# Matrix products of ones in TensorE's first waits, and three constant loads moved behind the tokens, in a two-layer hybrid decoder

## The chip, the cores and the metric

The kernel runs on one core of a Trainium2 chip. The metric is the device time of one execution in microseconds. A core has five engines that run their own instruction streams and wait for each other on semaphores: TensorE (PE in the profile; its weight loads have a row of their own, PEld), VectorE (DVE), ScalarE (ACT), GpSimd (POOL) and SyncE (SP). Copies between the memory of the device and the core are issued by SP, ScalarE or GpSimd and carried out by 16 DMA engines.

## The reference

Two layers of a decoder with 512 tokens behind 16 learned meta tokens, so 528 columns, and a model width of 1024. Each layer normalises its input, projects it, runs two kinds of heads side by side (forgetting attention, and retention with a fixed decay per head), joins them in an output projection, and ends with a gated feed-forward block:

```python
xn = rmsnorm(h, attn_norm_g)
proj = jnp.einsum('bld,dc->blc', xn, w_in)
fq, fk, fv, flog, rq, rk, rv, rg = jnp.split(proj, SPLIT_POINTS, axis=-1)
logf = jax.nn.log_sigmoid(flog.astype(jnp.float32) + b_fgate.astype(jnp.float32))
fox_out = fox_attention(fq.reshape(fshape), fk.reshape(fshape), fv.reshape(fshape), logf)
...
h = h + jnp.einsum('blc,cd->bld', mix, w_out)
hn = rmsnorm(h, ffn_norm_g)
ff = jax.nn.silu(jnp.einsum('bld,df->blf', hn, w_gate)) * jnp.einsum('bld,df->blf', hn, w_up)
return h + jnp.einsum('blf,fd->bld', ff, w_down)
```

Everything is float32. The change concerns the first 25 us or so of layer 0: the loads of the tokens, the first products of the input projection, the forget gates (`flog`) and the sum of squares of the norm.

## The kernel before, in words

**Layout.** The tokens stand transposed in eight tiles `h[0]` to `h[7]` of 128 features x 528 tokens. Weights come in tiles of 128 x 8 x 128, 512 KB each. To keep float32 accuracy with a faster number format, each operand is split into a high part and a low part (`xh`, `xl` of the tokens, `whi`, `wlo` of the weights), and each product is made of three: high by high, high by low, low by high (line 200). A product covers 264 columns, so there are six of them for each k (the 128 features) and each output tile. ScalarE makes the high parts (`xh` at line 298, `whi` at 176), VectorE or GpSimd the low ones (`xl` at 299, `wlo` at 177).

**The start of layer 0.** `start` (line 1096) issues all on SP: token tile 0, the first quarter of the two first weight tiles (those of q and k of the first pair of attention heads), token tile 1, the second quarter, token tiles 2 and 3, the other half of both weight tiles, token tiles 4 to 7. `scale_split` (line 290) then splits the tokens. Before that, at lines 52 to 59, four small constants are loaded: `idt` (a 128 x 128 identity for transposes) and `msk` (a 128 x 128 causal mask), 64 KB each, and `bfg` (the bias of the forget gates, 8 x 2) by GpSimd, and `vec` (norm weights) by ScalarE. `ones` (128 x 128) is written by VectorE at line 61; it serves as the weight operand that sums squares over the features.

**The order on TensorE** is written out by hand; `plan` is a list of steps, and `run(plan)` emits them under a manual schedule for TensorE alone. For layer 0 (line 1118) it alternates q and k: `qk[0]` is k = 0 of the q tile, `qk[1]` k = 0 of the k tile, and so on. After the first six of them come the squares of the tokens (`squares`, line 303; no TensorE work), then k = 3 to 6, then the forget gates (`forget_gates`, line 350: 32 products at line 360, with a split weight tile `pth` made from `wfr`), then the sums of squares (`col_rstd`, line 266: four products with `ones` at line 273, their results `R`), then `forget_sums` (line 369, which reads `bfg`, first through `nbfg` at line 373), and last k = 7. The v tile follows.

**The other engines** are ordered by the scheduler of the framework, which places every instruction by its own estimate of when its operands are there; an operand that arrives later moves its reader back in the stream of its engine. SP and GpSimd issue their DMAs in program order.

**PSUM.** `psum_a()` hands out four banks of 512 columns in turn, `psum()` two pairs.

Of the kernel before, what the change touches and what calls it, by code (L numbers as in the profile page):

```python
# [38 lines left out]
def hybrid_kernel(ctx, tc, x_t, w_in, w_fl, w_out, w_gate, w_up, w_down, vecs, b_fg, rope, decay, mask, ident, out_t):  # L39
    nc = tc.nc  # L40
# [9 lines left out]
    h = [state.tile([128, T], F32, name=f"h{k}") for k in range(NK)]  # L50

    idt = const.tile([128, 128], F32, name="idt")
    nc.gpsimd.dma_start(idt, ident)
    msk = const.tile([128, 128], F32, name="msk")
    nc.gpsimd.dma_start(msk, mask)
    vec = const.tile([128, vecs.shape[1]], F32, name="vec")
    nc.scalar.dma_start(vec, vecs)
    bfg = const.tile([FH, DEPTH], F32, name="bfg")
    nc.gpsimd.dma_start(bfg, b_fg)
    ones = const.tile([128, 128], F32R, name="ones")  # L60
    nc.vector.memset(ones.bitcast(F32), 1.0)
    epsc = const.tile([128, 1], F32, name="epsc")
# [35 lines left out]

    def zero(l, t):
        (nc.gpsimd if l else nc.vector).memset(t, 0.0)  # L100

    def take(lst, key):
        t = lst[rot[key] % len(lst)]
        rot[key] += 1
        return t
# [17 lines left out]
    def vcol(c):  # L123
        return vec[:, c:c + 1]
# [11 lines left out]
    def fetch(j):  # L136
        job = jobs[j]
        if "load" in job:
            job["load"]()
        elif "raw" not in job:  # L140
            n = job["src"].shape[1]
            job["raw"] = wp.tile([128, NK, 128], F32, name="raw", tag="raw", bufs=3)
            if j > 1:
                nc.sync.dma_start(job["raw"], job["src"]) if n == NK else \
                    nc.sync.dma_start(job["raw"][:, 0:n], job["src"])
# [96 lines left out]
    def psum_a():  # L242
        return psa.tile([128, 512], F32, name="psa", tag="psa")
# [5 lines left out]
    def tt(name, dt=F32):  # L249
        tag, bufs = tags[name]  # L250
        return tmp.tile([128, T], dt, name=name, tag=tag, bufs=bufs)

    def at(tag, dt=F32R, shape=(128, T), bufs=None):
        return phase["att"].tile(list(shape), dt, name=tag, tag=tag, bufs=bufs)
# [4 lines left out]
    def col_parts(src, cols):  # L259
        c_all = slice(cols[0][0], cols[-1][1])  # L260
        sh = tt("sqh", F32R)
        sl = tt("sql", F32R)
        split(sh[:, c_all], sl[:, c_all], src[:, c_all])
        return sh, sl
# [22 lines left out]
    FULL = ((0, HALF), (HALF, T))  # L287
    REAL = ((META, T),)

    def scale_split(st, gcol, cols):  # L290

        c = slice(cols[0][0], cols[-1][1])
        st["x"] = []
        for k in range(NK):
            xh = state.tile([128, T], F32R, name=f"xh{k}", tag=f"xh{k}")
            xl = state.tile([128, T], F32R, name=f"xl{k}", tag=f"xl{k}")
            g = vcol(gcol + k)
            nc.scalar.activation(xh[:, c], h[k][:, c], AF.Copy, scale=g)
            nc.vector.scalar_tensor_tensor(xl[:, c], h[k][:, c], g, xh[:, c].bitcast(F32),  # L299
                                           ALU.mult, ALU.subtract)  # L300
            st["x"].append((xh, xl))

    def squares(st, cols, pinned=False):
        c = slice(cols[0][0], cols[-1][1])
        acc = tt("ss")
        for k in range(NK):
            if k == 0:
                first = nc.scalar.activation(acc[:, c], h[0][:, c], AF.Square)
                if pinned:
                    tc.keep_in_program_order(first)  # L310
            else:
                sq = tt("sq")
                nc.scalar.activation(sq[:, c], h[k][:, c], AF.Square)
                nc.vector.tensor_add(acc[:, c], acc[:, c], sq[:, c])
        st["parts"] = col_parts(acc, cols)
# [23 lines left out]
    def rstd(st, cols, rname="R"):  # L339

        st["R"] = col_rstd(st["parts"], D, cols, rname)
# [27 lines left out]
    def forget_sums(l, st):  # L369
        z = st["z"]  # L370
        z2 = tt("z2")[0:FH]
        nbfg = tmp.tile([FH, 1], F32, name="nbfg", tag="nbfg")
        nc.vector.tensor_scalar_mul(nbfg, bfg[:, l:l + 1], -1.0)
        nc.vector.scalar_tensor_tensor(z, z, RSC, st["R"][0:FH, :], ALU.mult, ALU.mult)
        nc.scalar.activation(z2, z, AF.Abs, bias=bfg[:, l:l + 1])
        nc.scalar.activation(z2, z2, AF.Exp, scale=-1.0)
        nc.scalar.activation(z2, z2, AF.Ln, bias=onec[0:FH])
        nc.scalar.activation(z, z, AF.Relu, scale=-1.0, bias=nbfg)
        nc.vector.tensor_add(z, z, z2)
        nc.vector.tensor_tensor_scan(z2, z, z, 0.0, ALU.add, ALU.max)  # L380
        st["cdr"] = tc.dram_tile([FH, T], F32, name=f"cdr{l}")
        nc.sync.dma_start(st["cdr"], z2)
# [687 lines left out]
    def layer(l):  # L1070

        real = l == DEPTH - 1
        QC = REAL if real else FULL
        ly, ff = {}, {}
        fox = [{} for _ in range(FP)]
        ret = [{} for _ in range(RH)]

        def ropes():
            for i, n in enumerate(("cr", "sr")):
                t = at(n, F32)  # L1080
                nc.sync.dma_start(t, rope[i])
                nc.vector.scalar_tensor_tensor(t, t, RSC, ly["R"], ALU.mult, ALU.mult)
                ly[n] = t

        def fd(g):
            return fox_dense(l, g, ly, real, fox[g])

        def rd(hd, which):
            return ret_dense(l, hd, ly, real, ret[hd], which)

        mixes = [[fox[0], ret[0], fox[1], ret[1]], [fox[2], ret[2], fox[3], ret[3]]]
        fs = [fox_steps(g, fox[g], ly, real) for g in range(FP)]
        rs = [ret_steps(l, hd, ret[hd], real) for hd in range(RH)]
        plan = []

        def start():
            if l == 0:
                pieces = {0: (0, 2), 1: (2, 4), 3: (4, NK)}
                for k in range(NK):
                    nc.sync.dma_start(h[k], x_t[k])  # L1100
                    if k in pieces:
                        for j in range(2):
                            fetch(j)
                            c = slice(*pieces[k])
                            nc.sync.dma_start(jobs[j]["raw"][:, c], jobs[j]["src"][:, c])
            scale_split(ly, V_ATTN + l * NK, FULL)

        def start_ffn():
            scale_split(ff, V_FFN + l * NK, QC)

        q, k, v = fd(0)
        qk = [f for pair in zip(q, k) for f in pair]
        stats = [lambda: rstd(ly, FULL)]
        gates = [lambda: forget_gates(l, ly)]
        sums = [lambda: forget_sums(l, ly)]
        plan = [lambda: enter_att(l), start]
        if l == 0:
            plan += qk[:6] + [lambda: squares(ly, FULL, True)] + qk[6:-2] + gates + stats + sums + qk[-2:]
        else:
            plan += [lambda: squares(ly, FULL)] + q[:7] + stats + q[7:] + gates + sums + k  # L1120
        plan += v + [ropes]

        def ret_places(hd, *places):

            f = rs[hd]
            return list(zip(places, (f[0], f[1], f[2], f[4], f[3], f[5], f[6], f[7], f[8], f[9])))

        for g in range(2):
            main, rest = fs[g]
            m0, r0, places = (((7, 31), (34, 40.5), (13, 33.5, 35.5, 37.5, 39, 40.5, 43, 44, 47.5, 48)),  # L1130
                              ((0.5, 31.5), (32, 40), (13, 33.5, 35.5, 39.5, 39, 41.5, 43, 44, 47.5, 48)))[g]
            plan += merge(rd(g, "vqkg") + sum(fd(g + 1), []),
                          spread(main, *m0), spread(rest, *r0), ret_places(g, *places))
        main, rest = fs[2]
        op = out_proj(l, 0, mixes[0], real)
        op[:8] = op[0:3] + op[4:7] + [op[3], op[7]]
        plan += merge(op + sum(fd(3), []), spread(main, 4, 30.5), spread(rest, 32, 42))
        main, rest = fs[3]
        base = rd(2, "qkv") + rd(3, "qkv") + rd(2, "g") + rd(3, "g")
        op = out_proj(l, 1, mixes[1], real)  # L1140
        base += op[0:3] + op[4:7] + op[8:11] + op[12:15]
        plan += merge(base, spread(main, 2, 46.5), spread(rest, 51, 56),
                      ret_places(2, 26, 22.5, 23.5, 32, 28, 33.5, 36, 56.5, 40.5, 57.5),
                      ret_places(3, 52, 45.5, 47.5, 57.5, 55.5, 58.5, 60, 64.1, 63, 64.2))
        plan += [op[3], op[7], op[11], op[15]] + op[16:]
        up = ffn(l, ff, real, real)
        plan += [lambda: enter("ffn"), start_ffn] + up
        return plan

    plan = [f for l in range(DEPTH) for f in layer(l)]  # L1150
# [76 lines left out]
```

## Time and profile before

| | us |
|---|---|
| median of 3 runs | 1300.8 |
| lowest and highest | 1298.96, 1301.67 |
| profiled execution | 1302.07 |
| its span, first to last instruction | 1300.3 |
| TensorE busy in the span | 1271.6 |

The profile is of one execution. Its span is 1.8 us shorter than its time; what lies outside is start and end of the execution. A line of the timeline gives the start in us, the busy time, engine, source line, operation, output and inputs, shapes and count; instructions of one group that follow each other are merged, and in brackets stands the idle time ahead of them and what ended it. "PEq", "SPq" and so on are the sequencers, which issue DMAs and branch. In the chain that ended last, each line is a start, a length and who carried the chain in that time. In a table of windows, PEclk is the clock that was granted to TensorE, as a share of full speed. DMA queue q1 is the one of SP, q10 the one of ScalarE, and q0 (software) the one of GpSimd.

### The profile page before, as it was taken

The numbers are of one execution on the slowest core, as the hardware profiler recorded it, in microseconds if no ns is written. First come the engines' busy times: TensorE is split into PE (matmuls) and PEld (weight loads), VectorE is DVE, ScalarE is ACT, GpSimd is POOL, SyncE is SP. The second block draws the span as 40 slices with busy tenths as digits, with TensorE's granted clock in tenths as the row PEclk, the third lists the DMA queues.
The fourth block names the chain that finished last, engine by engine and source line by source line (L and its number), as shares of the span: only waits on it lengthen the run. The fifth ranks groups of instructions, "written<-read, shape, count | busy, mean of one in ns | idle before, by whom it ended". The sixth has DMA issues, their size and how long they took to land.

```text
span 1300.3 us, 23291 instructions
## 1 busy us (share of the span) xinstructions
PE 1271.6 (98%) x9326; PEld 1210.3 (93%) x9326; DVE 1005.5 (77%) x1827; ACT 706.7 (54%) x1277; POOL 192.7 (15%) x157
## 2 busy tenths in 40 slices
PE   8999999999999999999999999999999999999996
PEld 7999999999999999999998989988789999999995
DVE  7877756869988777777786767568899888888866
ACT  6776555576444444444466665457764444444444
POOL 3332333230000000000013324333200000000000
PEclk9999899999999999999999999999999999999998
DMA  5322222213333333332323222222224333333321
GB/s 196 107 76 72 74 82 82 60 55 122 103 110 98 98 98 98 98 98 82 102 71 115 74 82 82 77 87 66 97 81 129 99 98 97 98 111 103 96 65 65
DMA packets 45468, 120.54 MB, mean 93 GB/s; under 512 B 5376, under 2 KB 12032, under 8 KB 45360
## 3 DMA queue, kind: packets, MB, share of 16 engines
q1 hardware_dynamic: 45120, 118.90, 29.1%
q8 instruction: 73, 1.20, 0.4%
q14 instruction: 35, 0.29, 0.1%
q0 software_dynamic: 96, 0.13, 0.1%
q10 hardware_dynamic: 144, 0.02, 0.0%
HBM read 116.91 MB, written 2.13 MB: 92 GB/s over the span
## 4 chain that ended last, share of the span: by engine, by line
PE 82%; DVE 9%; ACT 6%; issue 1%; DMA 1%; POOL 0%; SPq 0%; DVEq 0%; ACTq 0%; POOLq 0%
PE psd L200 23%; PE psa L823 17%; PE psd L958 14%; PE psd L823 13%; PE psa L200 5%; PE psa L958 4%; PE psa L396 2%; PE psa L480 1%; PE psa L687 1%; PE psa L540 1%; DVE xl L299 1%; ACT whi L176 1%; PE psa L657 1%; DVE tq L585 1%; DVE ptl L129 1%
## 5 line engine op out<-in xcount | busy, mean ns | idle before, releaser
L177 POOL TENSOR_TENSOR wlo<-raw,whi 128x512 fp32r<-128x512 f32 x136 | 186.8, 1388 | 399.5 <-ACT whi L176 396.6
L200 PE MATMUL psd<-xh,whi 128*128 128x264 f32 (+1 forms) x792 | 198.0, 318 | 5.1 <-ACT whi L176 4.7
L200 PE MATMUL psd<-xh,wlo 128*128 128x264 f32 (+1 forms) x792 | 188.1, 305 | 0.4 <-POOL wlo L177 0.4
L200 PE MATMUL psd<-xl,whi 128*128 128x264 f32 (+1 forms) x792 | 188.0, 305 | 0.0
L200 PEld LDWEIGHTS psd<-xh,whi 128*128 128x128 f32 x792 | 130.2, 192 | 9.6 <-ACT whi L176 4.7
L200 PEld LDWEIGHTS psd<-xh,wlo 128*128 128x128 f32 x792 | 128.7, 191 | 6.5 <-POOL wlo L177 0.6
L200 PEld LDWEIGHTS psd<-xl,whi 128*128 128x128 f32 x792 | 129.3, 191 | 4.2 <-DVE xl L299 0.3
L176 ACT CAST whi<-raw 128x512 fp32r<-128x512 f32 (+1 forms) x170 | 99.6, 613 | 34.4 <-issue 17.8
L811 ACT CAST whi<-raw 128x1024 fp32r<-128x1024 f32 (+2 forms) x62 | 54.9, 885 | 49.8 <-PE psd L823 37.5
L811 ACT CAST fwhi<-raw 128x1024 fp32r<-128x1024 f32 (+2 forms) x62 | 55.7, 898 | 47.4 <-PE psd L823 39.7
L812 DVE TENSOR_TENSOR wlo<-raw,whi 128x1024 fp32r<-128x1024 f32 (+2 forms) x62 | 62.8, 1013 | 11.5 <-ACT whi L811 11.4
L812 DVE TENSOR_TENSOR fwlo<-raw,fwhi 128x1024 fp32r<-128x1024 f32 (+2 forms) x62 | 63.9, 1031 | 9.0 <-ACT fwhi L811 8.6
L823 PE MATMUL psa<-tl,whi 128*128 128x264 f32 (+1 forms) x232 | 65.8, 284 | 0.0
L823 PE MATMUL psa<-th,whi 128*128 128x264 f32 (+1 forms) x232 | 65.8, 284 | 0.0
L823 PE MATMUL psa<-th,wlo 128*128 128x264 f32 (+1 forms) x232 | 65.7, 283 | 0.0
L823 PE MATMUL psa<-th,fwhi 128*128 128x264 f32 (+1 forms) x224 | 63.6, 284 | 0.0
L823 PE MATMUL psa<-th,fwlo 128*128 128x264 f32 (+1 forms) x224 | 63.5, 283 | 0.0
L823 PE MATMUL psa<-tl,fwhi 128*128 128x264 f32 (+1 forms) x224 | 63.4, 283 | 0.0
L499 ACT ACTIVATE pdNone<-pdNone,nmax 128x144 f32<-128x144 f32 (+1 forms) x64 | 37.0, 577 | 47.9 <-DVE nmax L486 35.7
L129 DVE TENSOR_TENSOR ptl<-psa,pth 128x512 fp32r<-128x512 f32 (+4 forms) x88 | 41.8, 490 | 23.3 <-ACT pth L128 23.1
L811 ACT CAST fwhi<-S 128x1024 fp32r<-128x1024 f32 x20 | 21.0, 1051 | 69.7 <-PE psa L823 66.3
L889 ACT COPY e<-psa 128x264 f32<-128x264 f32 (+1 forms) x114 | 42.8, 375 | 27.7 <-PE psa L823 23.8
(311 smaller groups left out, 4035.7 us busy)
## 6 DMA issues: line engine op xcount, KB each, us to landing
raw<-w_in SPq DMA_DIRECT2D x54, 512.0 KB, 3.5
raw<-w_gate SPq DMA_DIRECT2D x44, 512.0 KB, 3.9
fraw<-w_up SPq DMA_DIRECT2D x38, 512.0 KB, 3.5
raw<-w_down SPq DMA_DIRECT2D x64, 256.0 KB, 2.9
raw<-w_out SPq DMA_DIRECT2D x16, 512.0 KB, 3.6
raw<-w_down SPq DMA_DIRECT2D x32, 192.0 KB, 2.5
bc<-cdr SPq DMA_DIRECT2D x16, 264.0 KB, 3.5
raw<-w_up SPq DMA_DIRECT2D x6, 512.0 KB, 3.4
```

The lines of the kernel that those rows point to most:

```text
L129: nc.vector.tensor_sub(lo, src, hi.bitcast(F32))
L176: nc.scalar.copy(hi, job["raw"][:, c0:c1])
L177: sub(lo, job["raw"][:, c0:c1], hi.bitcast(F32))
L200: nc.tensor.matmul(ps[1][b][:, 0:c1 - c0], w[:, wk, :], x[:, c0:c1], start=(k == 0 and i == 0), stop=(k == n - 1 and i == 2))
L299: nc.vector.scalar_tensor_tensor(xl[:, c], h[k][:, c], g, xh[:, c].bitcast(F32), ALU.mult, ALU.subtract)
L396: nc.tensor.transpose(ps[:, 128 * j:128 * j + 128], src[:, o:o + 128], idt)
L499: nc.scalar.activation(pr, pr, AF.Exp, bias=nmax[0:nq], scale=-1.0, accum_out=rsum)
L811: nc.scalar.copy(hi, src)
L812: nc.vector.tensor_sub(lo, src, hi.bitcast(F32))
L823: nc.tensor.matmul(bank()[:, 0:b.shape[-1]], a[:, o + k, :], b, start=(fresh and k == 0 and i == 0), stop=(k == n - 1 and i == 2), skip_gr ...
L889: nc.scalar.copy(self.t["e"][:, i], self.t["x"][:, 0:w])
L958: nc.tensor.matmul(v[:, 0:c1 - c0], a[:, s * n + k, :], b[:, c0:c1], start=(k == 0 and i == 0), stop=(k == n - 1 and i == 2))
```

## The change

Two things. First, a helper `keep_warm(n)` emits n products of `ones` by `ones`, 128 x 128 by 128 columns, into a PSUM bank of their own that nothing reads. 32 of them stand at the head of TensorE's stream, 16 between k = 0 and k = 1, and 4 between k = 1 and k = 2. Second, the loads of `idt`, `msk` and `bfg` leave GpSimd and the head of the program, and are issued by SP behind the eighth token tile, in the order `bfg`, `msk`, `idt`.

```diff
     idt = const.tile([128, 128], F32, name="idt")
-    nc.gpsimd.dma_start(idt, ident)
     msk = const.tile([128, 128], F32, name="msk")
-    nc.gpsimd.dma_start(msk, mask)
     vec = const.tile([128, vecs.shape[1]], F32, name="vec")
     nc.scalar.dma_start(vec, vecs)
     bfg = const.tile([FH, DEPTH], F32, name="bfg")
-    nc.gpsimd.dma_start(bfg, b_fg)
...
+    idle = []
+
+    def keep_warm(n):
+
+        if not idle:
+            idle.append(psum_a())
+        for _ in range(n):
+            nc.tensor.matmul(idle[0][:, 0:128], ones, ones, start=True, stop=True)
...
         def start():
             if l == 0:
+                keep_warm(32)
                 pieces = {0: (0, 2), 1: (2, 4), 3: (4, NK)}
...
+                for t, src in ((bfg, b_fg), (msk, mask), (idt, ident)):
+                    nc.sync.dma_start(t, src)
             scale_split(ly, V_ATTN + l * NK, FULL)
...
-            plan += qk[:6] + [lambda: squares(ly, FULL, True)] + qk[6:-2] + gates + stats + sums + qk[-2:]
+            plan += qk[:2] + [lambda: keep_warm(16)] + qk[2:4] + [lambda: keep_warm(4)] + qk[4:6] + [lambda: squares(ly, FULL, True)] + qk[6:-2] + gates + stats + sums + qk[-2:]
```

In the streams of the changed kernel, TensorE has the 52 products at these three places and is otherwise as before. GpSimd loses the three issues, SP gains them between the last token tile and the load of `wfr` (line 352). On VectorE the two `nbfg` (line 373) move from behind the first low weight part to between the additions of the squares (line 314); ScalarE's order is the same.

## The prediction

> **What bounds the kernel now.** I read the page first, then the waits and the chain of the first 45 us, then the timeline. The page's busy line and the shares of the chain that ended last:
>
> ```profile
> PE 1271.6 (98%) x9326; PEld 1210.3 (93%) x9326; DVE 1005.5 (77%) x1827; ACT 706.7 (54%) x1277; POOL 192.7 (15%) x157
> ...
> PE 82%; DVE 9%; ACT 6%; issue 1%; DMA 1%; POOL 0%; SPq 0%; DVEq 0%; ACTq 0%; POOLq 0%
> ```
>
> TensorE carries the span. The change touches only the first 24 us, so the question is by how much the work behind that point starts earlier or later. TensorE's longest wait from 0 to 45 us (total, times, longest), and the chain over the start:
>
> ```profile
> PE psd L200 <- ACT whi L176: 4.7, 1, 4.7
> ```
>
> ```profile
> 2.15 5.21 DMA h<-x_t
> ...
> 8.17 11.40 PE psd L200 x72
> 19.57 3.80 PE psa L360 x31
> ...
> 24.12 0.85 ACT R L278 x2
> ```
>
> The second token tile lands at 7.36 us. From 8.17 on TensorE itself is the chain: 72 products (k = 1 to 6), the forget gates (L360), the four sums of squares (L273). From 24.12 on ScalarE and VectorE carry it for a while (R, then q, k and the cumulated gates), and TensorE waits for them now and then. So whatever moves the L273 products moves all that follows by the same amount. In the timeline, the next product behind them starts at 23.79; that is my reference point.
>
> ```profile
> 0.83 0.17 DVE L61 MEMSET ones<- 128x128 f32 x1 [0.83 <-PEq L1215]
> ...
> 4.71 0.81 PE L200 MATMUL psd<-xh,whi 128*128 128x264 f32 x2 [4.71 <-ACT whi L176]
> ...
> 11.78 0.64 PE L200 MATMUL psd<-xl,whi 128*128 128x264 f32 x2
> ...
> 12.22 0.64 PE L200 MATMUL psd<-xh,wlo 128*128 128x264 f32 x2
> ...
> 13.08 0.41 PE L200 MATMUL psd<-xl,whi 128*128 128x264 f32 x2
> ...
> 13.33 0.40 PE L200 MATMUL psd<-xh,wlo 128*128 128x264 f32 x2
> ...
> 23.79 0.41 PE L200 MATMUL psd<-xh,whi 128*128 128x264 f32 x2
> ```
>
> Two products of 264 columns take 0.44 us before 12.9 us and 0.245 us after 13.1: 0.22 against 0.122 each. The array runs at half pace until about 13 us, and the released pace is what the added products are to bring forward.
>
> **The added products.** 32 stand ahead of the first real product, 16 behind the twelve of k = 0, 4 behind the twelve of k = 1. Each loads 128 columns of `ones` and streams 128. TensorE works in order, so the real ones wait for them. The trace has no such product; its nearest rows are 128-column transposes, at full and at half pace (each row asked for where one starts):
>
> ```profile
> 128.92 0.49 PE L396 MATMUL psa<-idt,pdNone 128*128 128x128 f32 x3
> 129.03 0.49 PE L396 MATMUL psa<-idt,pdNone 128*128 128x128 f32 x3
> ```
>
> ```profile
> 137.18 0.63 PE L548 MATMUL psa<-idt,tq 128*128 128x128 f32 x2
> 137.39 0.63 PE L548 MATMUL psa<-idt,tq 128*128 128x128 f32 x2
> ```
>
> Starts lie 0.11 us apart at full pace and 0.21 at half. By columns alone it would be 128/264 of 0.122 and 0.22, so 0.059 and 0.107; the weight load sets the pace. Products of 16 columns with a full weight load show it too:
>
> ```profile
> 133.49 0.28 PE L692 MATMUL psa<-rsh,rvh 128*128 128x16 f32 x1 [0.80 <-DVE ptl L129]
> 133.62 0.26 PE L692 MATMUL psa<-rsl,rvh 128*128 128x16 f32 x1
> ```
>
> (0.13 apart.) I take 0.11 and 0.213; the lower end, 0.107 at half pace, is kept for a rival. The Trainium skill (TensorE: Matmul & The Clock Gate, section on LDWEIGHTS) gives a load as its columns over 1.2 GHz whatever the clock, so 107 ns for 128 columns; the rows at full pace agree, those at half pace (0.21) do not, and by the page 32 products would end at 4.5 us and not at 7.9.
>
> **Do they release the clock?** This decides the case. The granted clock was 0.5 in one stretch in mid kernel, 135.9 to 142.7. The window just before it, two others, and the stretch itself (length; PE, PEld, DVE, ACT, POOL busy and count; PEclk; DMA):
>
> ```profile
> 132.50:135.91 3.41, 2.40 (x16) 2.07 (x15) 2.87 (x9) 1.60 (x4) 2.27 (x2) 1.00 0.59 177
> 770.80:774.20 3.40, 2.11 (x11) 1.15 (x9) 0.77 (x2) 3.33 (x6) 0.00 (x0) 1.00 0.48 154
> ...
> 6.21:9.62 3.41, 3.02 (x13) 2.41 (x12) 2.04 (x8) 2.23 (x5) 0.00 (x0) 1.00 1.03 370
> ```
>
> ```profile
> 135.90:142.70 6.80, 5.99 (x28) 5.88 (x27) 4.52 (x7) 2.19 (x6) 0.48 (x1) 0.50 0.34 108
> ```
>
> The stretch is 6.8 us long, twice 3.4, and begins 122.9 us, 36 times 3.41, behind the change of pace at 13.0: I read it as a decision every 3.41 us on the stretch just past, in a grid that does not start with the kernel. The clock fell behind the first window, in which PE and weight loads were busier (2.40, 2.07) than in the second (2.11, 1.15), where it held. Busy time and loads do not decide. Streamed columns do:
>
> ```profile
> L540 PE MATMUL psa<-pth,vv x5: 218/286/467, 134.4 to 135.7; 128*128 128x512 f32 x1, 128*128 128x400 f32 x1, 128*128 128x272 f32 x1, 128*128 128x144 f32 x1
> L540 PE MATMUL psa<-ptl,vv x5: 275/287/392, 134.7 to 135.8; 128*128 128x512 f32 x1, 128*128 128x400 f32 x1, 128*128 128x272 f32 x1, 128*128 128x144 f32 x1
> ```
>
> ```profile
> L200 PE MATMUL psd<-xh,whi 128*128 128x512 f32 x2 | 0.9, 437 | 0.0
> L200 PE MATMUL psd<-xh,wlo 128*128 128x512 f32 x2 | 0.8, 397 | 0.0
> L200 PE MATMUL psd<-xl,whi 128*128 128x512 f32 x2 | 0.8, 396 | 0.0
> L396 PE MATMUL psa<-idt,pdNone 128*128 128x128 f32 x4 | 0.7, 286 | 1.2 <-DVE sd L662 1.2
> ```
>
> The first window streams twice 1,344 columns (the fifth form has 16) and a few of 16, about 2,770; the second 6 x 512 + 4 x 128 less what began before it, about 3,300. At the start, 6.21 to 9.62 begins 11 products of 264, at most 2,900 columns, and the pace stayed at half (the PEclk column reads 1.00 there, but the pairs still take 0.44). At half pace 16 added products fit into 3.41 us: 16 x 128 = 2,050 columns, fewer than in any of these that fell or stayed. **So I take it that the added products alone do not release it**; dense real ones do (15 x 264 = 4,100 columns in 3.41 us).
>
> **The sum.** TensorE starts at 1.05, when `ones` is written. 32 x 0.213 = 6.8, so k = 0 starts at 7.9 and not at 4.71; its tokens and weights are there. 12 x 0.22 = 2.6: 10.5. Two paths from here. *Early*: these twelve release the clock at about 11.4. Of 16 added, 4 run at 0.213 and 12 at 0.11: 12.7. Then 12 x 0.122: 14.2; 4 x 0.11: 14.6; 60 x 0.122 for k = 2 to 6: 21.9; 32 x 0.122 for the gates: 25.8; 4 for the sums: 26.3. Against 23.79 that is 2.5 us later. *Late*: the added 16 dilute it, all run at 0.213 (13.9), and k = 1 releases it at about 15.9: 9 x 0.22 and 3 x 0.122 give 16.3, and the same rest (0.44 + 7.3 + 3.9 + 0.5) gives 28.4, 4.6 later. When in the 3.4 us grid the kernel starts is open, so both occur; between them, nearer the early one, I take 3.5 us later.
>
> **The moved loads.** Three software issues leave POOL; SP takes them behind the eighth token tile.
>
> ```profile
> q0 software_dynamic: 93, 0.13, 29.1%
> ```
>
> ```profile
> 3.00:4.00 1.00, 0.00 (x0) 0.00 (x0) 0.80 (x8) 0.37 (x1) 1.00 (x2) 1.00 1.10 224
> 4.00:5.00 1.00, 0.29 (x1) 0.29 (x2) 0.71 (x10) 0.66 (x2) 0.00 (x0) 1.00 0.72 180
> ...
> 6.00:7.00 1.00, 1.00 (x7) 1.00 (x6) 0.45 (x2) 0.04 (x1) 0.00 (x0) 1.00 1.04 361
> ```
>
> From 3 to 6 us the software queue took 29% of the engines' time, 0.87 us, and from 3 to 5 DMA moved 224 and 180 GB/s where it later moves 361. Without it the second token tile lands 0.9 to 2 us earlier. On my paths that is worth nothing: TensorE is not through the added products before 7.9, and ScalarE and VectorE are ahead of it from then on. If the added products were short, it would count in full (rival 2). The price of the move lies elsewhere:
>
> ```profile
> 6.98 0.14 DVE L373 TENSOR_SCALAR nbfg<-bfg 8x1 f32<-8x1 f32 x1 [0.49 <-DMA bfg<-b_fg]
> ...
> 8.75 0.52 SPq L352 DMA_DIRECT2D wfr<-w_fl  x1
> 9.44 3.37 SPq L144 DMA_DIRECT2D raw<-w_in  x2
> ...
> 16.64 0.23 ACT L128 CAST pth<-wfr 128x64 fp32r<-128x64 f32 x1
> ...
> 21.90 0.71 DVE L129 TENSOR_TENSOR sql<-ss,sqh 128x528 fp32r<-128x528 f32 x1 [0.70 <-ACT sqh L128]
> ```
>
> Three issues on SP at some 0.45 us move `wfr` from 8.75 to about 10.1; before, it was read 7.9 us after its issue, so it bears this, and the weight load that stands behind it waits in any case until 12.5 for a buffer. The two `nbfg` (0.14 each) move on VectorE between the additions of the squares: `sql` is ready at 22.9 instead of 22.6, and queued behind them are only those additions, L273's operands. L273 comes at 25.8, so 3 us of TensorE work cover it; without that cover it costs 0.3 us. Mask and identity serve the attention, behind R at 24.12. The other orders on VectorE, ScalarE and SP are unchanged, the spare PSUM bank makes no engine wait.
>
> **Rivals.**
> 1. *The added products do release the clock*, though they stream half the time. By mechanism: TensorE is never idle from 1.05 on, so the first whole window of 3.41 us ends between 4.5 and 7.9, and releases it. The 32 then end at 6.2 to 7.9; 12 x 0.122, 16 x 0.11, 12 x 0.122, 4 x 0.11, 60, 32 and 4 x 0.122 add 16.8: 23.0 to 24.7, that is 0.8 earlier to 0.9 later. Not slower: about 1300.8. For it: PE and weight loads without a gap. Against it: the two windows above. 22%. The Trainium skill (same page, Part 1 on the clock gate) states this rule: about 3.4 us of sustained issue release the clock, in a free-running window, whatever the number of products; the grid agrees with the rows here, that being busy suffices does not.
> 2. *Faster: the added products are short*, 0.107 at half pace. They end at 4.5, before the first operand, and the earlier tokens count. The real work then waits for VectorE: `sql` at 22.9 less 0.9 to 2, then four products; 0.9 to 2.6 us earlier, 1298.2 to 1299.9. It decides from the point where 32 of them take under 3.6 us (0.113 each). Against it: 0.21 in the L548 rows. 11%.
> 3. *No release before k = 2*: all through k = 1 and the 4 at half pace (17.4), release at about 22.2, 31.3 at the reference: 7.5 later, 1308.3. For it: 3.4 us with 2,050 columns on both sides of the twelve. 18%.
>
> **How the numbers follow.** The profiled execution took 1302.07 us (span 1300.3 and 1.8 around it), 1.3 above the median 1300.8; the half-pace stretch near 136 may be part of that, and it need not come in every run. I add the difference to the median: 1300.8 + 3.5 = **1304.3**, chance 46%, its own range 1302.8 to 1305.9. The remaining 3% is the unforeseen. The range from 1299.8 to 1308.6 takes in rivals 1 and most of 3, and the near end of 2. A difference of 0.2%, 2.6 us, is about what a measurement of this kernel can tell from no change. Slower by more: 30 of my 46 (the rest are early releases under 2.6), 18 of rival 3 and 2 of the rest, 50%. Faster by more: 5 of rival 2, and 5 for rivals 1 and 2 with a lucky clock in mid kernel, 10%. Within: 40%.
>
> **What would show it.** Right: 32 products of `ones` about 0.21 apart, the first L200 at 7.9, pairs at 0.44 through k = 0, release at 11 to 16, the first L200 behind L273 at 26 to 28.5. Wrong: pairs at 0.25 already in k = 0 (rival 1), the added ones 0.11 apart from the start (rival 2). The second token tile should land 0.9 to 2 us earlier with q0 empty, and nobody wait for `wfr`, `bfg`, mask or identity.

## The result, and the profile after

| | before | after |
|---|---|---|
| median of 16 runs each, side by side | 1300.11 us | 1303.16 us |
| lowest and highest | 1298.39, 1302.43 | 1301.44, 1306.04 |
| profiled execution, its span | 1302.07, 1300.3 | 1301.44, 1299.6 |

The ratio of after to before is 1.0026, with a 95% interval of 1.0019 to 1.0033. The changed kernel is 3.05 us slower, where 3.5 was forecast. (The 16 runs of before include the three from which 1300.8 came.)

The spans of the two profiled executions say the opposite: after's is 0.7 us shorter. The stage of the change must be read by itself. Here is TensorE's timeline after, over the first 26.5 us, with the lines that answer to those shown of before (L206 was L200, L279 was L273, L106 is the new helper):

```profile
1.05 7.09 PE L106 MATMUL psa<-ones 128*128 128x128 f32 x32 [1.05 <-DVE ones L58]
7.94 0.75 PE L206 MATMUL psd<-xh,whi 128*128 128x264 f32 x2
...
10.69 2.02 PE L106 MATMUL psa<-ones 128*128 128x128 f32 x16
12.54 0.46 PE L206 MATMUL psd<-xh,whi 128*128 128x264 f32 x2
...
14.05 0.56 PE L106 MATMUL psa<-ones 128*128 128x128 f32 x4
...
25.93 0.40 PE L279 MATMUL psa<-sql,ones 128*128 128x264 f32 x2
26.17 0.41 PE L206 MATMUL psd<-xh,whi 128*128 128x264 f32 x2
```

The 32 products take from 1.05 to 7.94, 0.215 each. The twelve of k = 0 take from 7.94 to 10.69, 0.229 each: still half pace. The 16 then take only 1.85 us, so the pace changes at their first or second (one at 0.213 and the rest at 0.11), at 10.9. The reference point, the first L206 behind the sums of squares, comes at 26.17 and not at 23.79: **2.4 us later**.

Where did the profiled execution get that back? The next two fences are the transposes near 137 us, where ScalarE had kept TensorE waiting, and the product behind that stage, first after, then before:

```profile
139.28 0.66 PE L554 MATMUL psa<-idt,tq 128*128 128x128 f32 x4 [0.83 <-ACT d L699]
...
143.46 0.49 PE L206 MATMUL psd<-xh,whi 128*128 128x264 f32 x2
```

```profile
136.91 1.12 PE L548 MATMUL psa<-idt,tq 128*128 128x128 f32 x4 [0.81 <-ACT d L693]
...
143.73 0.49 PE L200 MATMUL psd<-xh,whi 128*128 128x264 f32 x2
```

At the transposes after is still 2.37 us late, the whole of the 2.4. At the product behind them it is 0.27 early. Between them lies the stretch of 6.8 us in which before ran at half pace. The same window after:

```profile
135.90:142.70 6.80, 5.76 (x42) 5.53 (x43) 5.65 (x12) 3.53 (x9) 1.71 (x2) 1.00 0.55 190
```

The granted clock is 1.00 there. Before's profile lost 2.6 us to a fall of the clock that this execution was spared. Such falls come and go: in the profiles of the kernels below, one stood at 134.5, 136.8 or 142.2 us, or near 770, or there was none. So the two spans cannot be compared, and only the medians and the reference point can.

### The profile page after: what moved, and what is told of

Same layout as the page of the kernel before. It is cut to its first block, busy times and chain, and to the rows that moved or that the text cites. A ratio compares the mean times of both kernels' runs of the same rounds, so it can differ in the third digit from the quotient of the medians.

```text
span 1299.6 us, 23394 instructions
## 1 busy us (share of the span) xinstructions
PE 1275.3 (98%) x9378; PEld 1214.7 (93%) x9378; DVE 1006.1 (77%) x1827; ACT 706.8 (54%) x1277; POOL 190.8 (15%) x154
## 4 chain that ended last, share of the span: by engine, by line
PE 69%; DVE 5%; ACT 3%; issue 0%; DVEq 0%; ACTq 0%
PE psa L829 17%; PE psd L206 15%; PE psd L964 14%; PE psd L829 13%; PE psa L964 4%; PE psa L206 3%; PE psa L402 1%; DVE xl L305 1%; PE psa L486 1%; PE psa L693 1%; PE psa L546 0%; PE psa L663 0%; PE psa L279 0%; DVE tq L591 0%; ACT pdNone L505 0%
## 5 line engine op out<-in xcount | busy, mean ns | idle before, releaser
L206 PE MATMUL psd<-xh,whi 128*128 128x264 f32 (+1 forms) x792 | 196.2, 315 | 0.0
L206 PE MATMUL psd<-xh,wlo 128*128 128x264 f32 (+1 forms) x792 | 186.7, 303 | 0.4 <-POOL wlo L183 0.4
L206 PE MATMUL psd<-xl,whi 128*128 128x264 f32 (+1 forms) x792 | 186.2, 302 | 0.0
L206 PEld LDWEIGHTS psd<-xh,wlo 128*128 128x128 f32 x792 | 127.2, 189 | 6.4 <-POOL wlo L183 0.6
L206 PEld LDWEIGHTS psd<-xh,whi 128*128 128x128 f32 x792 | 128.5, 190 | 4.2
L206 PEld LDWEIGHTS psd<-xl,whi 128*128 128x128 f32 x792 | 127.8, 189 | 3.9
L818 DVE TENSOR_TENSOR fwlo<-raw,fwhi 128x1024 fp32r<-128x1024 f32 (+2 forms) x62 | 63.9, 1031 | 10.1 <-ACT fwhi L817 9.9
```

The source lines that it names most:

```text
L206: nc.tensor.matmul(ps[1][b][:, 0:c1 - c0], w[:, wk, :], x[:, c0:c1], start=(k == 0 and i == 0), stop=(k == n - 1 and i == 2))
L818: nc.vector.tensor_sub(lo, src, hi.bitcast(F32))
```

## The experiments

No experiment leaves out any of the computation; the products of ones are read by nothing. Each edit is shown against the changed kernel, except the second of experiment 4, which is shown against the kernel just ahead of it, and that of the last; dots mark code that is not shown. Each kernel is read by the reference point (23.79 before, 26.17 after) and, where it was timed, by its ratio to before.

**1. The two halves of the change, each alone.** The moved loads without a product:

```diff
-                keep_warm(32)
-            plan += qk[:2] + [lambda: keep_warm(16)] + qk[2:4] + [lambda: keep_warm(4)] + qk[4:6] + ...
+            plan += qk[:6] + ...
```

> The three constants are loaded behind the tokens, no product of ones is added. Theory (the added products cost their time in front of the real ones, the earlier tokens are hidden behind them): without them the earlier tokens count. The second token tile is split at about 6.1 us as in the changed kernel, the first product behind the sums of squares starts at 21.9 to 22.6 against 23.79, so 1.2 to 1.9 us faster than before, ratio 0.9985 to 0.9991. Rival (the moved loads are what made it slower, by queues or late constants): 1 us or more slower than before, ratio above 1.0008.

Median 1299.27, ratio 0.9994 (0.9985 to 1.0003); 0.9985 to 0.9991 was expected. The products without the moved loads:

```diff
+    nc.gpsimd.dma_start(idt, ident)
+    nc.gpsimd.dma_start(msk, mask)
+    nc.gpsimd.dma_start(bfg, b_fg)
...
-                for t, src in ((bfg, b_fg), (msk, mask), (idt, ident)):
-                    nc.sync.dma_start(t, src)
```

> The products of ones (32, 16, 4) are added, the loads stay on GpSimd at the head. Theory: TensorE is the bound from 1.05 us on, so it takes as long as the changed kernel: 2.4 to 4.6 us slower than before run by run, ratio 1.0022 to 1.0030, first real product at 7.9 us. Rival (the loads carry part of the loss): closer to before, ratio under 1.0015.

Median of 6 runs 1304.88, ratio 1.0034 (1.0022 to 1.0045), above the 1.0022 to 1.0030 that was expected. TensorE's timeline of the first kernel, then of the second:

```profile
4.90 0.81 PE L206 MATMUL psd<-xh,whi 128*128 128x264 f32 x2 [4.90 <-ACT whi L182]
...
9.53 0.41 PE L206 MATMUL psd<-xl,whi 128*128 128x264 f32 x2
...
21.68 0.51 PE L279 MATMUL psa<-sql,ones 128*128 128x264 f32 x2
22.03 0.41 PE L206 MATMUL psd<-xh,whi 128*128 128x264 f32 x2
```

```profile
10.69 2.38 PE L109 MATMUL psa<-ones 128*128 128x128 f32 x16
12.91 0.46 PE L209 MATMUL psd<-xh,whi 128*128 128x264 f32 x2
...
26.54 0.41 PE L209 MATMUL psd<-xh,whi 128*128 128x264 f32 x2
```

The loads alone bring the reference point 1.8 us forward, to 22.03, the products alone bring it to 26.54. The whole loss is that of the products. With them the loads bring almost nothing in the two traces: 26.17 against 26.54, and that is the place of the change of pace (10.9 against 11.7). The medians lie further apart, 1303.16 and 1304.88, and with six runs of the second kernel it stays open whether the loads have a part in that. Without the products, the 1.8 us of the trace show in the time as 0.9, too little to tell from none.

**2. Is it the columns or the time that releases the clock?** Same number of products and same weight loads, 256 columns each:

```diff
-            nc.tensor.matmul(idle[0][:, 0:128], ones, ones, start=True, stop=True)
+            nc.tensor.matmul(idle[0][:, 0:256].rearrange("p (a b) -> p a b", a=2), ones,
+                             ones.unsqueeze(1).broadcast_to([128, 2, 128]), start=True, stop=True)
```

> As the changed kernel, but each product of ones streams 256 columns instead of 128: the same number, the same weight loads, the same time at half pace, since 256 columns take what a weight load takes. Theory (streamed columns in 3.41 us release the clock): pace changes between 4.5 and 7.9 us, inside the first 32; the first real product starts at 6.2 to 7.9 and runs at full pace, the one behind the sums of squares at 23.0 to 24.7, ratio to before 0.9994 to 1.0007. Rival (being busy, or the number of products, releases it): as the changed kernel, release at 10 to 16, ratio 1.0020 to 1.0033.

```profile
1.05 5.42 PE L106 MATMUL psa<-ones 128*128 128x256 f32 x32 [1.05 <-DVE ones L58]
6.31 0.41 PE L207 MATMUL psd<-xh,whi 128*128 128x264 f32 x2
...
23.30 0.41 PE L207 MATMUL psd<-xh,whi 128*128 128x264 f32 x2
```

The timeline shows 32 products in 5.26 us instead of 6.89, and the pairs of k = 0 at 0.245 from the first on: twice the columns release the clock at about 4.1 us, sooner than the 4.5 that was expected as the earliest: the window that ended there began at 0.7, ahead of the first product, and its 14 products of 256 columns were enough. Median 1300.53, ratio 1.0003 (0.9994 to 1.0012): the loss is gone, and there is no gain. That the products of 128 columns keep TensorE as busy and load as many weights, and release nothing, rules out rival 1 of the prediction.

**3. Where does the threshold lie?** A measurement: 14 blocks of 64 products at the head of TensorE's stream, each block with its own number of columns, the loads moved as in the first experiment. (The loop over the blocks inside `keep_warm`, and the removal of the 16 and the 4, are not shown.)

```diff
...
-                keep_warm(32)
+                keep_warm((128, 160, 176, 192, 208, 224, 256, 128, 112, 104, 96, 88, 80, 64))
...
```

> A measurement of the clock: the loads behind the tokens, and at the head 14 blocks of 64 products of ones, with 128, 160, 176, 192, 208, 224, 256 columns, then 128, 112, 104, 96, 88, 80, 64; nothing reads them. At half pace a block lasts 13.6 us, four grids of 3.41. Theory (streamed columns, bounds from the trace of before: not released at 2,900, held at 3,300, fallen at 2,770 in 3.41 us): blocks of 128, 160 and 176 columns (2,050, 2,560, 2,820) stay 0.213 apart; release at 192 or 208 (3,070, 3,330); at full pace (0.11 apart) 128 and 112 hold (4,000, 3,500), and the clock falls at 104 to 88 (3,250 to 2,750). Rival (busy releases): products 0.11 apart already within the first block, from 4.5 to 7.9 us on, and no fall in any block, since TensorE is never idle.

The groups by form, from 1 to 146 us (busy time, mean ns of one):

```profile
L108 PE MATMUL psa<-ones 128*128 128x160 f32 x64 | 13.9, 415 | 0.0
L108 PE MATMUL psa<-ones 128*128 128x176 f32 x64 | 13.9, 415 | 0.0
...
L108 PE MATMUL psa<-ones 128*128 128x192 f32 x64 | 10.4, 341 | 0.0
L108 PE MATMUL psa<-ones 128*128 128x96 f32 x64 | 10.2, 334 | 0.0
...
L108 PE MATMUL psa<-ones 128*128 128x208 f32 x64 | 7.3, 275 | 0.0
...
L108 PE MATMUL psa<-ones 128*128 128x104 f32 x64 | 7.3, 274 | 0.0
```

A block takes 13.9 us at half pace (less the length of the last one, 13.5 / 63 = 0.214 apart) and 7.3 at full (7.03 / 63 = 0.112), whatever its columns, up to 176 at half pace and 208 at full: the weight load sets the pace in both. Its width does it: in before's trace, products of 16 columns start 0.026 us apart where the weights are 16 columns wide (three at 74.4 us), and 0.11 to 0.13 apart where they are 128 wide (from 133.49 on). The clock is released inside the block of 192 and falls inside the block of 96. The windows of 3.41 us around these two places (the PEclk column is no help before the first recorded change; the number of products tells the pace):

```profile
41.71:45.12 3.41, 3.41 (x18) 3.41 (x17) 0.00 (x0) 0.00 (x0) 0.00 (x0) 1.00 0.02 5
45.12:48.53 3.41, 3.41 (x18) 3.41 (x17) 0.00 (x0) 0.00 (x0) 0.00 (x0) 1.00 0.00 0
48.53:51.95 3.42, 3.42 (x32) 3.42 (x32) 0.00 (x0) 0.00 (x0) 0.00 (x0) 1.00 0.00 0
...
96.32:99.73 3.41, 3.41 (x33) 3.41 (x32) 0.00 (x0) 0.00 (x0) 0.00 (x0) 1.00 0.00 0
99.80:103.20 3.40, 3.40 (x18) 3.40 (x17) 0.00 (x0) 0.00 (x0) 0.00 (x0) 0.50 0.00 0
```

At half pace 16 products begin in a window (the count of 18 has those that reach over its ends). The first window holds 14 of 192 and 2 of 176, some 3,040 columns, and is not enough; the second holds 16 x 192 = 3,072, and behind it the clock is released. At full pace 3.41 / 0.1116 = 30.6 begin in a window: of 104 columns they are 3,180, and the clock stays; of 96 they are 2,940, and it falls. The window between these two holds both widths, some 3,150 columns, and the clock stays. TensorE is busy in every one of these windows without a gap. **Columns streamed in a window of 3.41 us decide: the clock is released at some 3,050 of them, and the fall lies between 2,940 and 3,150, so it can be the same number.** The 32 narrow products of the change stream 16 x 128 = 2,050.

The start of every kernel here agrees: counted back from the release in steps of 3.41 us, the window that ends there streams 3,072 to some 4,100 columns in all twelve traces, and no window before it more than 3,040. In mid kernel the count alone does not fit everywhere: two windows at half pace released the clock with some 2,890 and 2,970 columns (136.81 to 140.23 with the 32 products alone and 134.48 to 137.89 with the 16 and 4 alone, both in experiment 5), and two at full pace held it with some 2,700 and 2,800 (768.69 to 772.10 in experiment 2, 771.69 to 775.11 with the 32 products alone). Each of the four has four transposes of 128 columns in it; what a transpose counts for was not measured.

The Trainium skill (TensorE: Matmul & The Clock Gate, Part 1) lets about 3.4 us of sustained issue release the clock whatever the number of products, and an idle window throttle it. The windows agree on the 3.41 us and on a grid that runs by itself (51.2 us, 15 times 3.413, lie between the release at 48.53 and the fall at 99.73); on what is counted they differ, by the 41 us of gapless narrow products (1.05 to 42.1) that released nothing here and by the fall at 99.73 without an idle moment. The measurement decides.

**4. Is there a gain, if the release is cheap?** 16 products at the head and none between, of 256 columns by the edit of experiment 2 (not shown again); they end before the first operands come.

```diff
-                keep_warm(32)
+                keep_warm(16)
-            plan += qk[:2] + [lambda: keep_warm(16)] + qk[2:4] + [lambda: keep_warm(4)] + qk[4:6] + ...
+            plan += qk[:6] + ...
```

> Constants loaded behind the tokens, and 16 products of ones with 256 columns at the head only, which end at 4.5 us and so ahead of the first operand at 4.9. Theory: nothing real is delayed, the clock is released between 4.5 and 7.9 us, and the four sums of squares wait for VectorE (their last operand is ready at 21.6): product behind them at 21.9 to 22.1, against 22.03 with the moved loads alone in a run whose clock was released at 9.5, and up to 0.7 better than that where it is released late. Ratio to before 0.9984 to 0.9996. Rival (products of ones at the head always cost): slower than the moved loads alone by 0.5 us or more.

Median 1299.18, ratio 0.9993 (0.9984 to 1.0002), as with the moved loads alone. TensorE's timeline, then VectorE's:

```profile
7.51 0.51 PE L207 MATMUL psd<-xh,whi 128*128 128x264 f32 x2
8.32 0.51 PE L207 MATMUL psd<-xl,whi 128*128 128x264 f32 x2 [0.29 <-DVE xl L306]
...
22.00 0.51 PE L280 MATMUL psa<-sql,ones 128*128 128x264 f32 x2
22.35 0.41 PE L207 MATMUL psd<-xh,whi 128*128 128x264 f32 x2
```

```profile
16.73 0.70 DVE L321 TENSOR_TENSOR ss<-ss,sq 128x528 f32<-128x528 f32 x1
17.35 0.19 DVE L380 TENSOR_SCALAR nbfg<-bfg 8x1 f32<-8x1 f32 x2
17.47 3.07 DVE L321 TENSOR_TENSOR ss<-ss,sq 128x528 f32<-128x528 f32 x4
```

The clock is released at 6.4 instead of 9.5 and k = 1 begins at 7.51, yet the reference point is at 22.35, no earlier than the 22.03 of the moved loads alone. I had expected 21.9 to 22.1. TensorE now runs into ScalarE and VectorE. First it waits for high and low parts of the tokens, as at 8.32: between 7 and 13.5 us four steps from one product to the next are 0.33 to 0.58 us long where 0.122 is the pace, 1.3 us more in all. So the forget gates begin at 17.67, later than the 17.38 of the moved loads alone, which has no such step in that stretch. Then it waits for `sql`, which VectorE makes last, of the sum of the squares: the product with it begins at 22.00. With `sql` it was the same in the moved loads alone, and there VectorE's row shows it:

```profile
20.92 0.71 DVE L135 TENSOR_TENSOR sql<-ss,sqh 128x528 fp32r<-128x528 f32 x1 [0.70 <-ACT sqh L134]
```

`sql` ends at 21.63, and its product starts at 21.68. With the slower step behind it this costs 0.26 us: the four products of the sums take 0.74, against 0.48 in after, where nothing waits. As the two `nbfg` stand in the middle of these additions, I put the bias back on GpSimd at the head of the program:

```diff
+    nc.gpsimd.dma_start(bfg, b_fg)
...
-                for t, src in ((bfg, b_fg), (msk, mask), (idt, ident)):
+                for t, src in ((msk, mask), (idt, ident)):
```

> As the kernel with 16 wide products at the head, but the gate bias stays on GpSimd at the head, so that its two readers on VectorE leave the additions of the squares. Theory: these two (0.14 each) stand on what is now the bound; product behind the sums of squares 0.2 to 0.3 us earlier, 21.6 to 21.9. Rival (they stand on nothing): the same within 0.1, or later, if VectorE waits for the bias.

VectorE's timeline, and TensorE's at the reference point:

```profile
16.57 3.81 DVE L322 TENSOR_TENSOR ss<-ss,sq 128x528 f32<-128x528 f32 x5
```

```profile
22.20 0.41 PE L208 MATMUL psd<-xh,whi 128*128 128x264 f32 x2
```

The five additions take 3.81 us; with `nbfg` among them they took from 16.73 to 20.54, 3.81 as well. The reference point moves by 0.15, about as much as the start of the additions, and the ratio is 0.9994 (0.9985 to 1.0003). My expectation (21.6 to 21.9) failed: the place of `nbfg` costs nothing. The second addition has to wait for its square from ScalarE in both kernels: it starts 0.04 to 0.05 us after the square ends, with the `nbfg` ahead of it (17.42, 17.47) and without (17.27, 17.31).

**5. Which of the products cost what.** The 32 alone, and the 16 and 4 alone; one run each.

```diff
-            plan += qk[:2] + [lambda: keep_warm(16)] + qk[2:4] + [lambda: keep_warm(4)] + qk[4:6] + ...
+            plan += qk[:6] + ...
```

> The changed kernel with the 32 products of 128 columns at the head alone, without the 16 and the 4. Theory: first real product at 7.94, k = 1 at 10.7; release at 10 to 14; product behind the sums of squares at 24.0 to 25.2, so 0.2 to 1.4 later than before, and 2 to 3.2 later than the moved loads alone. The 16 and 4 then cost the remaining 1 to 2 us of the changed kernel.

```profile
10.62 0.40 PE L206 MATMUL psd<-xh,whi 128*128 128x264 f32 x2
...
23.78 0.41 PE L206 MATMUL psd<-xh,whi 128*128 128x264 f32 x2
```

```diff
-                keep_warm(32)
```

> The changed kernel without the 32 at the head, with the 16 and the 4. Theory: first real product at 4.9 as with the moved loads alone, k = 0 ends at 7.7 at half pace, the 16 run to 11.1 at half pace or, where k = 0 released the clock, to 9.6; product behind the sums of squares at 23.2 to 25.3. Rival (products in a wait are free): 22.0 to 22.3 as with the moved loads alone.

```profile
7.71 2.13 PE L106 MATMUL psa<-ones 128*128 128x128 f32 x16
9.68 0.46 PE L206 MATMUL psd<-xh,whi 128*128 128x264 f32 x2
...
23.33 0.41 PE L206 MATMUL psd<-xh,whi 128*128 128x264 f32 x2
```

Both timelines stand against the 22.03 of the moved loads alone: the 32 cost 1.75 us, the 16 and 4 cost 1.3. The first was a little less than expected (24.0), as k = 0 released the clock at 10.5. The 16 are issued at 7.71, right behind k = 0. With the moved loads alone, k = 1 began there at 7.77 without a wait, so this run does not say whether products in a wait would be free.

Together the two parts would give 3.05; after lies 4.14 behind 22.03. The traces add up without any effect of one part on the other. The 32 put off the first real product by 3.04 (7.94 against 4.90); the 16 and the 4 take 1.97 and 0.40 here, 1.85 and 0.40 in after. In all three kernels the clock is then released after 12 real products, where the moved loads alone ran 21 at half pace: 9 x 0.098 = 0.9 back. And in none of the three does TensorE wait for `sql`, which costs the moved loads alone 0.26. So after has 3.04 + 2.25 - 0.9 - 0.26 = 4.1, and the two parts taken singly have each had both deductions.

**6. Can the late path be forced?** The prediction left open when in the grid the kernel starts. The same 52 products, with 12 of the 16 put between the q half and the k half of k = 0, so that no window is dense before k = 1:

```diff
-            plan += qk[:2] + [lambda: keep_warm(16)] + qk[2:4] + ...
+            plan += qk[:1] + [lambda: keep_warm(12)] + qk[1:2] + [lambda: keep_warm(4)] + qk[2:4] + ...
```

> The changed kernel with the same products in another order: of the 16, 12 stand between the q half and the k half of k = 0, and 4 behind it. Theory (about 3,000 columns in one 3.41 us release the clock, as the blocks showed): the six real products on each side, 1.32 us, are too few beside products of 128 columns, so the release comes at the first grid point behind 14.2, up to 17.7, in place of 10.9; k = 1 starts at 14.0 and the product behind the sums of squares at 27.7 to 29.3, so 1.5 to 3.1 us later than in the changed kernel with not one product more; ratio to before 1.0035 to 1.0055. Rival (the amount of work decides, not where it stands): 26.2 to 26.6 and ratio 1.0019 to 1.0033, as the changed kernel.

```profile
9.37 2.65 PE L106 MATMUL psa<-ones 128*128 128x128 f32 x12
11.82 0.75 PE L206 MATMUL psd<-xh,whi 128*128 128x264 f32 x2
...
15.42 0.64 PE L206 MATMUL psd<-xh,whi 128*128 128x264 f32 x2
...
16.15 0.40 PE L206 MATMUL psd<-xh,wlo 128*128 128x264 f32 x2
...
28.52 0.28 PE L206 MATMUL psd<-xh,whi 128*128 128x264 f32 x1
```

The timeline shows half pace until 15.9, and the reference point at 28.52, 2.35 later than after with not one product more. The windows that end at 9.1 and 12.5 stream some 2,600 columns each, the one that ends at 15.9 some 3,600. Four runs, median 1305.57 (1305.32 to 1305.97), ratio 1.0043 (1.0026 to 1.0059). So a later release alone costs about as much here as the whole change did in after's profile (2.38).

**7. Only mask and identity moved**, from the kernel before, with the bias left on GpSimd and no products:

```diff
-    nc.gpsimd.dma_start(idt, ident)
-    nc.gpsimd.dma_start(msk, mask)
...
+                for t, src in ((msk, mask), (idt, ident)):
+                    nc.sync.dma_start(t, src)
```

> The kernel before with mask and identity loaded behind the tokens, the bias where it was, and no product of ones. Theory: the moved 128 KB are all that helps; the product behind the sums of squares comes at 21.9 to 22.6 as with all three loads moved, release at 8 to 12, ratio to before 0.9985 to 0.9998. Rival (the earlier tokens are worth nothing by the end of the kernel): ratio 0.9998 to 1.0005.

```profile
8.01 0.41 PE L198 MATMUL psd<-xl,whi 128*128 128x264 f32 x2
...
22.13 0.41 PE L198 MATMUL psd<-xh,whi 128*128 128x264 f32 x2
```

Release at 8.0 without any product of ones, reference point at 22.13, median 1299.64, ratio 0.9996 (0.9987 to 1.0005): not to be told from before. Its interval reaches into both the expected range and that of the rival, so the time does not decide between them. Before's profile is itself one draw of the grid: with the release at 13.0 all of its k = 1 ran at half pace, here hardly any of it did. That the 1.7 us of the trace show as 0.4 in the medians may come from this; it was not tested with further profiles of before. No version tried here beats the kernel before by more than the measurement can tell.

## Why the prediction was right

**What bounds the kernel, and the reference point.** Right. The shift at the reference point was still whole at 139 us, 2.37 of 2.38. It holds for a shift forward too: with the moved loads alone, 1.8 at the reference point is 2.0 at 131 us.

**The length of the added products.** Right: 0.215 at half pace against 0.213, first real product at 7.94 against 7.9. Their width does not matter up to 176 columns (experiment 3), and rival 2, short products, fell.

**No release by the added products alone.** Right, and with the right reason: columns. Experiments 2 and 3 show it by changing the columns alone. The two windows that it was read from were thinner ground: the one that held has four transposes in it, and the count of 2,770 in the one that fell goes by starts and leaves out the rest of a product of 512 columns that began at 132.30, just ahead of it. (15 x 264 is 3,960; the 4,100 is for the 15.5 products that fit into 3.41 us.)

**The sum.** The early path came: release at 10.9 against 11.4, reference point 26.17 against 26.3. The late path was not in the profile, but experiment 6 makes it: 28.52 against 28.4. The threshold of 3,050 gives an estimate of how often it should come by itself. A window of 15.75 products must hold 264 n + 128 (15.75 - n) columns, so n = 7.6 real ones, 1.7 us of them. k = 0 lasts 2.75. If a window's end cuts it between 1.05 and 1.7 us behind its start, neither part is enough: 0.65 of 3.41 us, 19% of the starts.

Of after's 16 runs 13 lie between 1301.44 and 1304.44 and three between 1305.81 and 1306.04, where the forced late path lies; three of 16 are 19%. That those three are late paths is argued from their time, as no trace of them is on record. A fall of the clock in mid kernel does not explain them: their mean granted clock is 0.994, as in the four forced runs, and four more of after's runs with 0.994 lie at 1302.96 to 1303.53, some 2.7 us lower. That the share is 19% both times is partly luck: of the six runs with the products alone (experiment 1), two lie at 1305.9 and 1306.1 with the same clock.

With 81% of 2.4 and 19% of 28.52 - 23.79 = 4.7, the mean shift is 2.8, and 3.05 was measured; both shifts are taken from one profile of before, whose own place in the grid varies. The forecast of 3.5 was a choice between 2.5 and 4.6, not a sum, and put the weight too far towards the late path.

**Rival 3**, no release before k = 2, was priced too high at 18%: none of the 16 runs lies near its 1308.3. By the same count, a start that cuts k = 0 badly cuts k = 1 (6.05 us later, 0.77 less than two windows) between 1.82 and 2.47 us, and that is enough. The row it rested on, 3.4 us of 2,050 columns on both sides of the twelve, was right, but a window needs 1.7 us of real products, and not 3.4. (Rival 2's sum has a slip: `sql` at 20.9 to 22.0 and four products of 0.122 come 1.3 to 2.4 us ahead of 23.79, not 0.9 to 2.6. The moved loads alone, without any product, came 1.8 ahead.)

**The moved loads.** The time was right, a part of the reasons wrong. The second token tile, here by its first reader in ScalarE's timeline, after and then before:

```profile
6.07 0.73 ACT L304 ACTIVATE xh<-h,vec 128x528 fp32r<-128x528 f32 x1 [0.36 <-DMA h<-x_t]
```

```profile
7.39 0.73 ACT L298 ACTIVATE xh<-h,vec 128x528 fp32r<-128x528 f32 x1 [1.35 <-DMA h<-x_t]
```

And the windows of DMA's dip, after:

```profile
3.00:4.00 1.00, 1.00 (x7) 1.00 (x7) 0.23 (x2) 0.23 (x1) 0.00 (x0) 1.00 1.07 230
4.00:5.00 1.00, 1.00 (x7) 1.00 (x6) 1.00 (x9) 0.80 (x2) 0.00 (x0) 1.00 0.68 194
```

It comes 1.3 us earlier, as forecast (0.9 to 2), and on the path after nobody needs it. But the dip to 224 and 180 GB/s, which I had put down to the software queue, is still there without that queue, at 230 and 194. The tile is earlier because 128 KB stand in front of it no more, or because the order of the packets differs; no run tells these apart, and what makes the dip stays open. `nbfg` was to cost 0.3 us without its cover; without it (experiment 4) it cost nothing. `sql`, put at 22.9, is ready at 21.64 after, since the tokens that it is made from came earlier; four us of cover hid that. `wfr` is issued at 10.63 and not at 10.1. Nothing after waits for the rest: TensorE has no wait at all between 12 and 26 us, and mask and identity, issued at 9.1 and 10.0, are first read at 41 and 43 us.

**Where the intended gain went.** The half pace from 4.7 to 13 us in before looked like the thing to gain. At the reference point the profile with the moved loads alone is 1.8 us ahead. Some 1.1 of it is the second token tile (the wait for it at 7.36 us and the slow steps right behind), and 1.1 the pace, 21 real products at half pace against 32; the later first product takes back 0.2, and `sql` 0.26. The place of the release is a draw of the grid, so the second part need not come from the loads; but a release as early in before could not bring its reference point much under 23.0, as its `sql` ends at 22.61. Beyond that, ScalarE and VectorE stand in the way: kernels that release the clock at 9.5, 6.4 and 4.5 (experiments 1 and 4) reach the reference point at 22.03, 22.35 and 22.20. What an earlier release gains is lost in waits for the parts of the tokens, and at the end for `sql`.

## What to carry to other kernels

A product that is to warm up the array must stream columns: count those of a window of 3.41 us (here it took some 3,050), and see that the filler ends before the first operand comes, since TensorE works in order and each product beyond that is a delay. Before buying a faster clock for a stage, look at what arrives last once TensorE is early (here the parts of the tokens and the squares, from ScalarE and VectorE): it caps the gain. And where the clock falls now and then in mid kernel, compare stages and medians, not the spans of two profiles.

## What the runs showed of the hardware

The granted clock follows the columns that TensorE streamed in the last window of 3.41 us. With plain products the release takes some 3,050 of them (more than 3,040, at most 3,072), and the clock falls somewhere between 3,150 and 2,940, so that a TensorE that never idles falls below it if its products are narrow beside their weight loads. In windows with transposes the clock was released or held with fewer, down to some 2,700, and why was not settled. The load of a 128 x 128 float32 weight sets a product's pace, 0.214 us at half clock and 0.112 at full, as long as it streams no more than 176 and 208 columns (the widest forms of one pace in experiment 3 at each clock that are shown); with weights of 16 columns, products of 16 columns start 0.026 us apart at full clock. What makes DMA dip between 3 and 5 us of the kernel was not settled.
